# A decoder trunk on one core: gate evacuations ahead of recurrences, forget gate on ScalarE, scores times values first, the last norm later, two output rows stored first

## The chip, the cores and the metric

The kernel runs on one core of a Trainium2 chip, in one launch. The metric is the device time in microseconds (us) of one execution, as the median of several runs. PE is TensorE (PEld its weight loads), DVE is VectorE, ACT is ScalarE, POOL is GpSimd; SP issues nearly all DMAs.

## The reference

Sequence 2048, width 1024, batch 1, one layer, float32:

```python
proj = (rms_norm(x) * (1 + sc1) + sh1) @ w_in          # 3856 columns, cut into groups of heads:
#   retention (4 heads), HGRN2 (8 heads), GLA (4 heads); each a chunkwise recurrence, chunks of 64
f     = lb + (1 - lb) * sigmoid(z)                     # HGRN2: forget gate
key   = (1 - lb) * sigmoid(-z)                         # HGRN2: key
o     = (scores * causal decay) @ v + (q * decay) @ S  # per chunk: inside the chunk, and from the state S
S     = decay * S + (k * decay).T @ v
o     = rms_norm(o) per head * silu(gate)
x     = x + g1 * (concat(o) * head_gain @ w_out)
h     = rms_norm(x) * (1 + sc2) + sh2
u     = causal_conv3(h @ w_up)                         # 2 x 2816 columns
x     = x + g2 * ((silu(u_gate) * u_val) @ w_down)
out   = rms_norm(x) * final_gain
```

The scales sc, shifts sh and gates g come from a conditioning vector.

## The kernel before

Features lie on the partitions, tokens on the free axis. Matmuls are full precision by three passes: each operand is split into a high and a low part (`high` and `low`, `split`: a CAST on ACT, then a subtraction on DVE), and `split3` multiplies high by high, high by low, low by high; in the profile these are L254, L255 and L256. (In the changed kernel every line from here on has a number one to ten higher.)

**Token mixer.** Four blocks b = 0..3 of 512 tokens. In each, seven units follow one another: four of HGRN2 (`unit_h`, h0 to h3, tiles named like `kh1_3` for block 1, unit 3), one of GLA (`unit_g`), two of retention (`unit_r`). A unit is projections (`cf_gemm`, `tf_gemm`, `tf512`: tiles `psh..`, `psvg..`, `psqkvgr`), their evacuation from PSUM to SBUF by ACT and DVE, and then a recurrence (`gated`, `retention`), whose small matmuls are spread between the projections of later units. For HGRN2 `sf` and `sn` are the two sigmoids, `f` the forget gate, `kq` the key (tile `kh`), `sq` the silu of q (`sqh`), `v`/`sg` value and silu gate (`tok_evac`, `tok_evac4`, tiles `vh`, `sgh`, `sgg`). The recurrence scales q and k level by level (`qbh`, `kh`, `eh`), makes scores (`lvh`, `ath`), the output `oh` (`attn_out`: state product first, then scores times values, chunk by chunk) and updates states `S` from `uh`. For the retention units the scores are `scrr` and `atr`, the output `or`.

The next block's norm is three parts: `norm1_stat` sums squares (`san`), `rstd` transposes the sum by PE (`ssn`), takes the inverse root on DVE with three Newton rounds (12 tiny operations, `rsn`) and broadcasts it by PE (`bcn`), and `norm1_h` scales the rows (`xn`) and splits them into `ha`. After the mixer `out_half` and `out_finish` multiply by w_out (tiles `y`), add to the residual rows `x1` and make the second norm (`n2`), whose rows go to DRAM as `h2d`. For the last block these rows are normed in place: the four two-row buffers (`xy`) of `x1_3` are stored and then pass to the FFN.

**FFN.** Two super-blocks of 1024 tokens, with seven products instead of eight in each 2 x 2 split (Strassen's scheme). `up_stage` makes for each of 22 column groups f the products into PSUM tiles X, Y, Z (operands `A` from weights, `B` from features, the last-made ones `hB`/`lB`), adds them up to `uv` and `ug` (a ring `u` of three buffers), takes the convolution (`yv`, `yg` in the four `xy` buffers) and the gate. `up_second` of group f is issued inside group f+1. `down_stage` multiplies by w_down; `down_norm` makes the final norm of a half, and then scales and stores row by row; rows `y` 6 and 7 of half 0 lie in buffers (`t2s`) that the next super-block's weights also use.

**What sets the order.** PE executes in the order in which the program issues its matmuls. That order is made by `Clock`: each projection moves a clock on (`adv`), and generators and callbacks (`at(us, fn)`, `chain(gen, us)`) are run when it reaches their due time. So a number such as 14.0 says after how much PE work something is issued. The order on DVE, ACT and the queues is made by a scheduler that goes by priorities: `tc.high_priority(offset=...)` puts instructions ahead by that much; HOT is 600, CHAIN is 400. On each engine the order is then fixed, and an instruction waits for its operands and holds up all behind it.

## Time and profile before

| | us |
|---|---|
| median of 3 runs | 2531.41 (2528.41 to 2534.57) |
| profiled execution, its own time | 2533.2 |
| its span (first to last instruction) | 2531.4, mean granted clock 0.992 |
| PE busy | 2452.0 (97%) |
| DVE busy | 1989.5 (79%) |
| ACT busy | 1147.5 (45%) |
| POOL busy | 146.3 (6%) |

The mixer takes the first 1240 us or so, the up stage of super-block 0 begins there. A wait in the profile is put down to the instruction that ended it. Stretches are given in us from the start of the span. A group line reads: line, engine, operation, out<-in, count, then busy us, mean ns of one, and idle time ahead of it. "PEclk" or granted clock is 1.00 at full speed.

### The profile page before, as it was taken

The numbers are of one execution on the slowest core, as the hardware profiler recorded it, in microseconds if no ns is written. First come the engines' busy times: TensorE is split into PE (matmuls) and PEld (weight loads), VectorE is DVE, ScalarE is ACT, GpSimd is POOL, SyncE is SP. The second block draws the span as 40 slices with busy tenths as digits, with TensorE's granted clock in tenths as the row PEclk, the third lists the DMA queues.
The fourth block names the chain that finished last, engine by engine and source line by source line (L and its number), as shares of the span: only waits on it lengthen the run. The fifth ranks groups of instructions, "written<-read, shape, count | busy, mean of one in ns | idle before, by whom it ended". The sixth has DMA issues, their size and how long they took to land.

```text
span 2531.4 us, 35178 instructions
## 1 busy us (share of the span) xinstructions
PE 2452.0 (97%) x12165; PEld 2059.3 (81%) x12165; DVE 1989.5 (79%) x3652; ACT 1147.5 (45%) x1950; POOL 146.3 (6%) x278
## 2 busy tenths in 40 slices
PE   5999999999999999999999999999989999999998
PEld 4888877888888888788788888888868888888887
DVE  8987887877688685877798888887678777778666
ACT  3334434434443434434554454455445545545442
POOL 1000000000000000000100000000001010010000
PEclk9999999999999999999999999999999999999999
DMA  8844458865689647884654544587665544447663
GB/s 312 296 159 134 169 169 322 290 234 169 215 283 318 224 157 241 311 300 158 222 190 147 171 147 141 168 283 243 209 199 186 159 137 152 150 133 263 213 196 126
DMA packets 232498, 525.11 MB, mean 207 GB/s; under 512 B 24928, under 2 KB 28032, under 8 KB 232320
## 3 DMA queue, kind: packets, MB, share of 16 engines
q1 hardware_dynamic: 229120, 512.38, 60.0%
q0 software_dynamic: 3200, 10.49, 1.2%
q8 instruction: 96, 1.57, 0.2%
q14 instruction: 82, 0.67, 0.1%
HBM read 397.46 MB, written 125.30 MB: 207 GB/s over the span
## 4 chain that ended last, share of the span: by engine, by line
PE 82%; DVE 8%; DMA 5%; issue 2%; ACT 1%; SPq 0%; DVEq 0%; POOL 0%; ACTq 0%; POOLq 0%
PE X L254 6%; PE X L256 6%; PE X L255 6%; PE Z L256 3%; PE Z L255 3%; PE Z L254 3%; PE lvh L662 3%; PE dX L256 3%; PE dX L255 3%; PE dX L254 3%; PE psqkvgr L254 2%; PE psqkvgr L256 2%; PE psqkvgr L255 2%; PE y L254 2%; PE y L256 2%
## 5 line engine op out<-in xcount | busy, mean ns | idle before, releaser
L254 PE MATMUL X<-B,A 128*128 128x512 f32 x572 | 224.4, 392 | 1.4 <-ACT u L1354 1.4
L255 PE MATMUL X<-B,A 128*128 128x512 f32 x572 | 223.9, 391 | 0.0
L256 PE MATMUL X<-B,A 128*128 128x512 f32 x572 | 223.6, 391 | 0.0
L1055 DVE TENSOR_TENSOR dA<-rd,dA 128x512 fp32r<-128x512 f32 x154 | 106.0, 689 | 87.6 <-ACT dA L1054 87.5
L1054 ACT CAST dA<-rd 128x512 fp32r<-128x512 f32 x154 | 95.6, 621 | 138.8 <-PE dY L256 42.2
L1055 DVE TENSOR_TENSOR A<-s,A 128x512 fp32r<-128x512 f32 x176 | 120.7, 686 | 40.7 <-ACT A L1054 40.3
L1054 ACT CAST A<-s 128x512 fp32r<-128x512 f32 x176 | 108.6, 618 | 68.0 <-PE Z L256 45.2
L254 PE MATMUL dX<-dB,dA 128*128 128x512 f32 x352 | 136.9, 389 | 0.0
L255 PE MATMUL dX<-dB,dA 128*128 128x512 f32 x352 | 136.9, 389 | 0.0
L256 PE MATMUL dX<-dB,dA 128*128 128x512 f32 x352 | 136.9, 389 | 0.0
L254 PEld LDWEIGHTS X<-B,A 128*128 128x128 f32 x572 | 108.2, 189 | 24.5 <-ACT u L1354 2.2
L255 PEld LDWEIGHTS X<-B,A 128*128 128x128 f32 x572 | 108.2, 189 | 22.7
L256 PEld LDWEIGHTS X<-B,A 128*128 128x128 f32 x572 | 108.2, 189 | 22.7
L255 PE MATMUL Z<-B,A 128*128 128x512 f32 x308 | 120.0, 390 | 2.2 <-DVE B L1055 2.2
L254 PE MATMUL Z<-B,A 128*128 128x512 f32 x308 | 119.9, 389 | 0.0
L256 PE MATMUL Z<-B,A 128*128 128x512 f32 x308 | 119.8, 389 | 0.0
L662 PEld LDWEIGHTS lvh<-qbh,kh 128*128 128x128 f32 x768 | 100.5, 192 | 17.0 <-issue 9.2
L1055 DVE TENSOR_TENSOR dB<-rb,dB 128x512 fp32r<-128x512 f32 x154 | 105.6, 686 | 10.2 <-ACT dB L1054 10.1
L1055 DVE TENSOR_TENSOR A<-r,A 128x512 fp32r<-128x512 f32 x130 | 89.3, 687 | 29.4 <-ACT A L1054 29.1
L662 PE MATMUL lvh<-qbh,kh 128*128 128x128 f32 x768 | 102.8, 277 | 7.3 <-DVE kh L672 7.1
L1054 ACT CAST A<-r 128x512 fp32r<-128x512 f32 x130 | 81.0, 623 | 62.4 <-PE Z L256 60.0
L254 PE MATMUL psqkvgr<-hqkvgr,ha 128*128 128x512 f32 x256 | 106.1, 415 | 1.1 <-DVE orsg L160 1.0
(475 smaller groups left out, 6981.2 us busy)
## 6 DMA issues: line engine op xcount, KB each, us to landing
gs<-yv SPq DMA_DIRECT2D x154, 256.0 KB, 2.9
rb<-gs SPq DMA_DIRECT2D x154, 256.0 KB, 3.9
r<-wup SPq DMA_DIRECT2D x140, 256.0 KB, 3.3
s<-sumsu SPq DMA_DIRECT2D x136, 256.0 KB, 3.0
wada<-wada SPq DMA_DIRECT2D x48, 512.0 KB, 6.0
rd<-sumsd SPq DMA_DIRECT2D x88, 256.0 KB, 3.8
rd<-wdown SPq DMA_DIRECT2D x66, 256.0 KB, 3.9
x<-xT SPq DMA_DIRECT2D x64, 256.0 KB, 5.8
```

Of the source, the lines that this page charges most:

```text
L254: T.matmul(ps, lhs[0], rhs[0], start=first, stop=False, skip_group_check=more)
L255: T.matmul(ps, lhs[0], rhs[1], start=False, stop=False, skip_group_check=more)
L256: T.matmul(ps, lhs[1], rhs[0], start=False, stop=last, skip_group_check=more)
L662: T.matmul(ps[:, c * P:(c + 1) * P].rearrange("p (h n s) -> p h n s", h=2, s=s), kq[:, c * P:(c + 1) * P], rhs, start=True, stop=True)
L1054: S.copy(hi, src)
L1055: V.tensor_tensor(lo, src, hi, op=ALU.subtract)
```

## The change

1. The evacuations of projections (values, gates, the q sigmoid and its multiply, GLA's and retention's copies) get priority HOT.
2. `f` and `kq` of `unit_h` are made by ACT (a scaled activation each) instead of DVE: 32 instructions move.
3. `attn_out` multiplies scores by values for all chunks first, then adds the state products.
4. `norm1_h` gets priority CHAIN, and `norm1_stat` issues its sum after 20 us of PE work instead of 14.
5. The recurrence chains of `unit_h` begin after 9 (unit 0 of blocks 0 and 1) or 7 instead of 9 (block 0, unit 0) or 6.
6. For the last block, the squares of the second norm get priority -100 instead of 600, and the sum is issued at 20 instead of 5.
7. `down_norm` scales and stores rows 6 and 7 first in half 0, and the broadcast comes after 9 or 13 instead of 8 or 10.

```diff
+LATER = 100
...
         # norm1_stat
-                clock.at(14.0, rstd(acc[0], f"n1_{b}", bc1[b][:], lambda: done.add(("n1", b)), gap=9.5))
+                clock.at(20.0, rstd(acc[0], f"n1_{b}", bc1[b][:], lambda: done.add(("n1", b)), gap=9.5))
...
         # norm1_h
-            scaled(t[:], bc1[b][:], k)
-            high(t[:], k, f"{b}_")
-            low(t[:], k)
+            with tc.high_priority(offset=CHAIN):
+                scaled(t[:], bc1[b][:], k)
+                high(t[:], k, f"{b}_")
+                low(t[:], k)
...
         # tok_evac, and in the same way tok_evac4, sf and sn, sq, al, kq, qs and z of unit_g, a of unit_r
-            S.copy(v[:, c2, :], p3[:, :, 0:P])
-            S.activation(sg[:, c2, :], p3[:, :, P:256], AF.Sigmoid)
-            V.tensor_tensor(sg[:, c2, :], sg[:, c2, :], p3[:, :, P:256], op=ALU.mult)
+            with tc.high_priority(offset=HOT):
+                S.copy(v[:, c2, :], p3[:, :, 0:P])
+                S.activation(sg[:, c2, :], p3[:, :, P:256], AF.Sigmoid)
+                V.tensor_tensor(sg[:, c2, :], sg[:, c2, :], p3[:, :, P:256], op=ALU.mult)
...
         # attn_out
         for c in range(NCH):
-            oc = ps[:, c * P:(c + 1) * P]
-            inter = not (b == 0 and c == 0)
-            if inter:
-                T.matmul(oc, qn[:, c * P:(c + 1) * P], Sst[:, (b * NCH + c) % NS, :], start=True, stop=False)
             for hh in range(2):
-                T.matmul(oc[:, hh * 64:hh * 64 + 64], attn[:, (c * 2 + hh) * P:(c * 2 + hh + 1) * P],
-                         v[:, c, hh * 64:hh * 64 + 64], start=not inter, stop=hh == 1 if inter else True)
+                T.matmul(ps[:, c * P + hh * 64:c * P + hh * 64 + 64], attn[:, (c * 2 + hh) * P:(c * 2 + hh + 1) * P],
+                         v[:, c, hh * 64:hh * 64 + 64], start=c == hh == 0, stop=False, skip_group_check=True)
+        for c in range(1 if b == 0 else 0, NCH):
+            T.matmul(ps[:, c * P:(c + 1) * P], qn[:, c * P:(c + 1) * P], Sst[:, (b * NCH + c) % NS, :],
+                     start=False, stop=c == NCH - 1, skip_group_check=True)
...
         # unit_h
-        V.tensor_scalar(f[:], sf[:], oml[:, u:u + 1], lb[:, u:u + 1], op0=ALU.mult, op1=ALU.add)
-        V.tensor_scalar(kq[:], sn[:], oml[:, u:u + 1], None, op0=ALU.mult)
+        S.activation(f[:], sf[:], AF.Identity, scale=oml[:, u:u + 1], bias=lb[:, u:u + 1])
+        S.activation(kq[:], sn[:], AF.Copy, scale=oml[:, u:u + 1])
...
-        clock.chain(gated(nm, b, u, pos, kq, decay, subs, xy), 9.0 if b == u == 0 else 6.0)
+        clock.chain(gated(nm, b, u, pos, kq, decay, subs, xy), 9.0 if u == 0 and b < 2 else 7.0)
...
         # out_half
-                    with tc.high_priority(offset=HOT):
+                    with tc.high_priority(offset=HOT if b < NB - 1 else -LATER):
                         sumsq(acc, x1[m], m, f"n2_{b}_")
...
         # out_finish
-        clock.at(5.0, rstd(acc, f"n2_{b}", bc[:], then, gap=9.5))
+        clock.at(5.0 if b < NB - 1 else 20.0, rstd(acc, f"n2_{b}", bc[:], then, gap=9.5))
...
         # down_norm
-        def then(m=0):
+        def then(n=0):
+            m = (n - 2) % KD if h == 0 else n
...
-        clock.at(7.0 if h else 12.0, rstd(acc, f"n3_{b}", bc[:], then, bank=bank, gap=8.0 if h else 10.0))
+        clock.at(7.0 if h else 12.0, rstd(acc, f"n3_{b}", bc[:], then, bank=bank, gap=9.0 if h else 13.0))
```

Three places show how it moves instructions. The first is DVE in unit h3 of block 0, around 174 us of the trace. Here `kg`, `qbg`, `atg` are GLA's recurrence, `eh0_2` and `fh0_2` the decays of unit h2, `san` the sum of squares for the next block. Before:

```order
L626 TENSOR_TENSOR eh0_2_1441<-fh0_2_1440 128x128
L359 TENSOR_TENSOR san1_1_1450<-san1_1_1450,sqn1_1_5_1646 128x512
L626 TENSOR_TENSOR eh0_2_1441<-eh0_2_1441 128x64
L744 TENSOR_SCALAR fh0_3_1629<-sfh0_3_1689,oml_89,lb_90 128x512
L626 TENSOR_TENSOR eh0_2_1441<-eh0_2_1441 128x32
L745 TENSOR_SCALAR kh0_3_1628<-snh0_3_1690,oml_89 128x512
L626 TENSOR_TENSOR eh0_2_1441<-eh0_2_1441 128x16
L359 TENSOR_TENSOR san1_1_1450<-san1_1_1450,sqn1_1_6_1705 128x512
L626 TENSOR_TENSOR eh0_2_1441<-eh0_2_1441 128x8
L749 TENSOR_TENSOR sqh0_3_1771<-pshqh0_3_1708,sqh0_3_1771 128x512
L626 TENSOR_TENSOR eh0_2_1441<-eh0_2_1441 128x4
```

and after:

```order
L360 TENSOR_TENSOR san1_1_1450<-san1_1_1450,sqn1_1_5_1646 128x512
L759 TENSOR_TENSOR qbh0_2_1615<-sqh0_2_1606,fh0_2_1440 64x512 x2
L317 TENSOR_TENSOR lvgh0_3_2_1900<-rvgh0_3_2_1897,hvgh0_3_2_1899 128x1024
L754 TENSOR_TENSOR sqh0_3_1771<-pshqh0_3_1708,sqh0_3_1771 128x512
L673 TENSOR_TENSOR qbg0_0_1156<-qbg0_0_1156,eg0_991 128x64x8
L673 TENSOR_TENSOR qbg0_1_1165<-qbg0_1_1165,eg0_991 128x64x8
L675 TENSOR_TENSOR kg0_989<-kg0_989,eg0_991 128x32x8
L684 COPY_PREDICATED atg0_0_1590<-m_all_87,lvg0_8_1756 128x64x8
L684 COPY_PREDICATED atg0_1_1592<-m_all_87,lvg0_8_1761 128x64x8
L629 TENSOR_TENSOR eh0_2_1441<-fh0_2_1440 128x128
L360 TENSOR_TENSOR san1_1_1450<-san1_1_1450,sqn1_1_6_1705 128x512
L629 TENSOR_TENSOR eh0_2_1441<-eh0_2_1441 128x64
```

The multiply `sqh0_3`, which is what empties its PSUM bank, stood behind the decay chain `eh0_2` and the last GLA scores, and now stands ahead of both, and f and kh of unit h3 (L744, L745) are gone from this engine.

The second is DVE at the border from block 1 to block 2, around 584 us: `S3_110` is the state of unit h3, which PE reads for `oh1_3`; `xn2`, `ha2` are the next block's rows; `x1_1_0` a residual row; `ra1r` and `kkr` belong to retention. Before:

```order
L365 SCALAR_TENSOR_TENSOR xn2_0_5507<-xn2_0_5507,mod_104,bc1_2_4662 128x512
L853 TENSOR_TENSOR ra1r1_1_5444<-ra1r1_1_5444,rb1r1_1_5446 128x8x32
L854 TENSOR_TENSOR ra1r1_1_5444<-ra1r1_1_5444,rb1r1_1_5446 128x8x32
L372 SCALAR_TENSOR_TENSOR ha2_0_5510<-xn2_0_5507,mod_104,ha2_0_5510 128x512
L711 SCALAR_TENSOR_TENSOR S3_110<-S3_110,eh1_3_4444,uh1_3_5596 64x64
L986 SCALAR_TENSOR_TENSOR x1_1_0_5561<-y1_0_1_5586,mod_104,x1_1_0_5561 128x512
L711 SCALAR_TENSOR_TENSOR S3_110<-S3_110,eh1_3_4444,uh1_3_5596 64x64 x7
L365 SCALAR_TENSOR_TENSOR xn2_1_5513<-xn2_1_5513,mod_104,bc1_2_4662 128x512
```

and after:

```order
L714 SCALAR_TENSOR_TENSOR S3_110<-S3_110,eh1_3_4444,uh1_3_5593 64x64 x2
L366 SCALAR_TENSOR_TENSOR xn2_0_5507<-xn2_0_5507,mod_104,bc1_2_4662 128x512
L366 SCALAR_TENSOR_TENSOR xn2_1_5513<-xn2_1_5513,mod_104,bc1_2_4662 128x512
L996 SCALAR_TENSOR_TENSOR x1_1_0_5561<-y1_0_1_5586,mod_104,x1_1_0_5561 128x512
L366 SCALAR_TENSOR_TENSOR xn2_2_5519<-xn2_2_5519,mod_104,bc1_2_4662 128x512
L373 SCALAR_TENSOR_TENSOR ha2_0_5510<-xn2_0_5507,mod_104,ha2_0_5510 128x512
L373 SCALAR_TENSOR_TENSOR ha2_1_5516<-xn2_1_5513,mod_104,ha2_1_5516 128x512
L373 SCALAR_TENSOR_TENSOR ha2_2_5522<-xn2_2_5519,mod_104,ha2_2_5522 128x512
L714 SCALAR_TENSOR_TENSOR S3_110<-S3_110,eh1_3_4444,uh1_3_5593 64x64 x6
L866 TENSOR_TENSOR kkr1_1_5233<-ra1r1_1_5444,c_all_86 128x512
```

The first two of eight state updates come ahead of the rows of the next block now, and seven 128x512 operations stand between them and the other six.

The third is the beginning of the up stage, around 1262 us. On PE, `bcn2_3` is the broadcast of the last block's second norm. Before:

```order
L255 MATMUL Z0_0_11726<-B0_3_1_11713,A0_0_3_11624 128x512
L256 MATMUL Z0_0_11726<-B0_3_1_11713,A0_0_3_11624 128x512
L348 MATMUL bcn2_3_11872<-c_all_86,rsn2_3_11767 128x128 x4
L254 MATMUL Z0_0_11726<-B0_3_2_11718,A0_0_3_11624 128x512
L255 MATMUL Z0_0_11726<-B0_3_2_11718,A0_0_3_11624 128x512
L256 MATMUL Z0_0_11726<-B0_3_2_11718,A0_0_3_11624 128x512
```

and after:

```order
L255 MATMUL X0_2_11988<-B0_1_3_11012,A0_2_1_11950 128x512
L256 MATMUL X0_2_11988<-B0_1_3_11012,A0_2_1_11950 128x512
L257 MATMUL X0_2_11988<-B0_1_3_11012,A0_2_1_11950 128x512
L349 MATMUL bcn2_3_12010<-c_all_86,rsn2_3_11899 128x128 x4
L255 MATMUL X0_1_11810<-B0_4_0_11688,A0_1_4_11803 128x512
L256 MATMUL X0_1_11810<-B0_4_0_11688,A0_1_4_11803 128x512
L257 MATMUL X0_1_11810<-B0_4_0_11688,A0_1_4_11803 128x512
```

It stood in product 3 of column group 0 (`Z0_0`), and now stands behind a product of group 2 and ahead of product 4 of group 1 (`X0_1`, 12 matmuls), which product 3 of group 1 (`Z0_1`) follows. On DVE at the same place, `x1_3` are the normed rows, `yv0_0` and `yg0_0` the convolution of group 0, `ug0_1` the sum that reads `Z0_1`. Before:

```order
L1055 TENSOR_TENSOR A0_2_6_12005<-s1_0_2_11995,A0_2_6_12005 128x512
L1011 SCALAR_TENSOR_TENSOR x1_3_4_11200<-x1_3_4_11200,mod_104,bc2_3_11661 128x512 x2
L1011 SCALAR_TENSOR_TENSOR x1_3_6_11304<-x1_3_6_11304,mod_104,bc2_3_11661 128x512
L1055 TENSOR_TENSOR A0_2_5_12008<-s0_0_2_11994,A0_2_5_12008 128x512
L1011 SCALAR_TENSOR_TENSOR x1_3_6_11304<-x1_3_6_11304,mod_104,bc2_3_11661 128x512
L1277 TENSOR_TENSOR s2_0_2_11996<-r00_0_2_11984,r10_0_2_11998 128x512
L1289 SCALAR_TENSOR_TENSOR yv0_0_11917<-uv0_0_11727,vec_84,yv0_0_11917 128x1024
L1055 TENSOR_TENSOR A0_2_7_12012<-s2_0_2_11996,A0_2_7_12012 128x512
L1290 SCALAR_TENSOR_TENSOR yv0_0_11917<-uv0_0_11727,vec_84,yv0_0_11917 128x1024
L1280 TENSOR_TENSOR s3_0_2_11997<-r01_0_2_11986,s1_0_2_11995 128x512
L1355 TENSOR_TENSOR ug0_1_11834<-Z0_1_11832,u3_0_1_11839 128x512
```

and after:

```order
L1065 TENSOR_TENSOR A0_3_2_12157<-r01_0_3_12152,A0_3_2_12157 128x512
L1021 SCALAR_TENSOR_TENSOR x1_3_0_11041<-x1_3_0_11041,mod_104,bc2_3_11661 128x512 x2
L1021 SCALAR_TENSOR_TENSOR x1_3_2_11095<-x1_3_2_11095,mod_104,bc2_3_11661 128x512 x2
L1021 SCALAR_TENSOR_TENSOR x1_3_4_11191<-x1_3_4_11191,mod_104,bc2_3_11661 128x512
L1065 TENSOR_TENSOR A0_2_3_11981<-s3_0_2_11959,A0_2_3_11981 128x512
L1021 SCALAR_TENSOR_TENSOR x1_3_4_11191<-x1_3_4_11191,mod_104,bc2_3_11661 128x512
L1021 SCALAR_TENSOR_TENSOR x1_3_6_11304<-x1_3_6_11304,mod_104,bc2_3_11661 128x512 x2
L1299 SCALAR_TENSOR_TENSOR yv0_0_11859<-uv0_0_11727,vec_84,yv0_0_11859 128x1024
L1300 SCALAR_TENSOR_TENSOR yv0_0_11859<-uv0_0_11727,vec_84,yv0_0_11859 128x1024
L1299 SCALAR_TENSOR_TENSOR yg0_0_11865<-ug0_0_11728,vec_84,yg0_0_11865 128x1024
L1365 TENSOR_TENSOR ug0_1_11814<-Z0_1_11812,u3_0_1_11819 128x512
```

The rows stand in one piece directly ahead of the convolution, with one operand split among them, and `ug0_1` stands behind one more step of the convolution.

## The prediction

> **What bounds the kernel now.** I read the page first, then the waits of PE, then stretches around each wait, then single instructions. All times are those of the profiled execution: 2533.2 us, of which the span is 2531.4 and 1.8 lie around it. The median of the runs is 2531.41, 1.8 below it, so I form the change against 2533.2 and take the same difference off the median.

> ```profile
> PE 2452.0 (97%) x12165; PEld 2059.3 (81%) x12165; DVE 1989.5 (79%) x3652; ACT 1147.5 (45%) x1950; POOL 146.3 (6%) x278
> PE 82%; DVE 8%; DMA 5%; issue 2%; ACT 1%; SPq 0%; DVEq 0%; POOL 0%; ACTq 0%; POOLq 0%
> ```

> PE works 2452.0 of 2531.4 us and no matmul is added or removed, so all that can change is the 79 us in which PE is not busy, and the stretches in which its clock is halved. The waits of PE (waiting instruction <- releaser: us in total, times, longest us; the 14.6, 3.9, 3.7 and 2.7 of the startup are left out, the change doesn't touch them):

> ```profile
> PE lvh L662 <- DVE kh L672: 7.1, 6, 3.8
> PE X L254 <- ACT A L1054: 6.2, 2, 5.1
> PE pshfh L254 <- DVE sgg L561: 4.5, 1, 4.5
> ...
> PE psvgh L254 <- DVE sqh L749: 3.7, 1, 3.7
> PE X L254 <- ACT hB L1054: 2.7, 1, 2.7
> ...
> PE ssn L337 <- DVE S L711: 2.6, 1, 2.6
> ...
> PE Z L255 <- DVE B L1055: 2.2, 1, 2.2
> PE bcn L348 <- DVE rsn L160: 2.0, 1, 2.0
> PE pshfh L255 <- DVE ha L372: 1.9, 1, 1.9
> ...
> PE psqkvgr L254 <- DVE orsg L160: 1.0, 1, 1.0
> ...
> PE alg L790 <- DVE sgh L561: 0.6, 1, 0.6
> ```

> Each is one place, except kh (six). The stretches around them, with the busy time of PE, PEld, DVE, ACT and POOL, then the granted clock:

> ```profile
> 172.00:186.00 14.00, 10.34 (x42) 8.68 (x41) 11.85 (x26) 1.68 (x2) 0.00 (x0) 0.76 0.43 141
> 300.00:314.00 14.00, 12.11 (x58) 10.15 (x56) 9.56 (x28) 5.45 (x8) 1.04 (x2) 0.88 0.42 142
> 340.00:350.00 10.00, 6.53 (x32) 6.02 (x33) 9.01 (x18) 0.84 (x2) 0.00 (x0) 0.83 0.33 107
> 578.00:600.00 22.00, 22.00 (x125) 19.12 (x124) 21.05 (x56) 11.11 (x19) 2.08 (x4) 1.00 0.73 244
> 600.00:880.00 280.00, 277.08 (x1532) 237.19 (x1530) 213.70 (x509) 116.11 (x223) 9.38 (x18) 1.00 0.71 244
> 880.00:900.00 20.00, 20.00 (x133) 18.16 (x132) 19.01 (x46) 10.07 (x17) 2.08 (x4) 1.00 0.51 174
> 1040.00:1052.00 12.00, 7.55 (x25) 5.75 (x24) 8.02 (x24) 2.95 (x11) 0.00 (x0) 0.72 0.76 256
> 1246.00:1262.00 16.00, 13.29 (x46) 10.06 (x47) 11.49 (x29) 8.43 (x16) 3.36 (x6) 0.79 0.61 204
> 1860.00:1900.00 40.00, 31.12 (x130) 23.79 (x129) 28.87 (x63) 13.68 (x24) 5.17 (x11) 0.96 0.58 191
> ```

> Two things are to be seen. A wait costs more than itself: the clock falls after it, and length times (1 - clock) is lost besides, 14 x 0.24 = 3.4 us at 172, 12 x 0.28 = 3.4 at 1040, 16 x 0.21 = 3.4 at 1246, 1.7 at 300 and at 340, 1.6 at 1860. And at the borders between blocks (578 to 600, 880 to 900) PE is 100% busy while DVE is busy 96% and 95%: there is no wait, and no room on DVE for one to be avoided.

> **What the change takes away.** *At 177* the gate multiply sqh is late:

> ```profile
> 170.88 0.60 ACT L748 ACTIVATE sqh<-pshqh 128x512 f32<-128x512 f32 x1
> 176.36 0.69 DVE L749 TENSOR_TENSOR sqh<-pshqh,sqh 128x512 f32<-128x512 f32 x1
> 177.10 0.80 PE L254 MATMUL psvgh<-hvgh,ha 128*128 128x512 f32 x1 [3.66 <-DVE sqh L749]
> ```

> Its sigmoid ended at 171.5 and DVE came to it 4.9 us later; that held a PSUM bank that PE needs. At priority HOT it stands ahead of the recurrence work. The wait of 3.7 and the 3.4 of clock go: **-7.0**. *At 1045* sgg holds a bank in the same way (12.00 - 7.55 = 4.45, and 3.4): **-7.8**. *At 1886* an activation tile of the next super-block is cast late because its buffer still holds rows 6 and 7 of the output, stored last; now they go first. Idle in 1860 to 1900 is 40.00 - 31.12 = 8.9, of it 2.0 the norm's wait (its broadcast comes some 3 us later, so that goes too); I leave 0.7, and 1.6 of clock goes: **-9.8**. *At 309* 1.9 + 1.7: **-3.6**. *At 343* (kh, 3.5 and 1.7) DVE is 9.01 of 10 busy and only about 1 us of its work leaves for ACT, so of a possible 5.2 I take **-1.0**. *The smaller ones* (S 2.6, orsg 1.0, the other five of kh 7.1 - 3.8 = 3.3, and 0.6) have either later steps on PE or earlier ones on DVE: 7.5, of which I take **-6.5**. Sum: -35.7.

> **Forget gate and key on ScalarE.**

> ```profile
> L744 DVE TENSOR_SCALAR fh<-sfh,oml,lb 128x512 f32<-128x512 f32 x16 | 8.7, 542 | 3.1 <-ACT sfh L742 3.0
> L1012 ACT ACTIVATE x<-x,mod 128x512 f32<-128x512 f32 x8 | 5.7, 720 | 1.2 <-DVE x L1011 1.1
> ```

> Sixteen f (0.54 each) leave DVE, and sixteen kh of nearly the same length, some 16 us in all. The nearest row for them on ACT is a scaled ACTIVATE of the same shape, 0.72: 32 x 0.72 = 23 us on an engine that is 45% busy, with no more tables to load. Their wait is bounded by 0 and by 16 x (0.72 - 0.54) = 3; I take 0, since the chain behind them is DVE work that is queued anyway. Scores times values first costs PE no instruction and moves the read of the state some 2 us later in each chunk group; nothing by itself.

> **What the change puts in.** *Borders.* norm1_h of the next block is at CHAIN now, so its 16 DVE operations (xn, ha) stand ahead of what PE waits for there: the last states S, and the retention scores.

> ```profile
> L372 DVE SCALAR_TENSOR_TENSOR ha<-xn,mod,ha 128x512 fp32r<-128x512 f32 x24 | 17.7, 745 | 0.2
> 585.68 2.16 DVE L711 SCALAR_TENSOR_TENSOR S<-S,eh,uh 64x64 f32<-64x64 f32 x7
> 586.55 0.38 PE L594 MATMUL oh<-S,qbh 128*128 128x128 f32 x2
> 598.20 0.69 DVE L903 TENSOR_TENSOR atr<-scr,c_all 128x512 f32<-128x512 f32 x1
> 600.25 0.38 PE L594 MATMUL or<-S,qnr 128*128 128x128 f32 x2
> ```

> Before, PE read S while the updates ran, and the second half of atr ended 1.4 us ahead of its reader. Now seven 128x512 operations (six of norm1_h, one of the residual; some 0.66 each as they overlap, 4.6 in all) stand between the second update of S and the third, and the rest of norm1_h ahead of atr. Two operations that stood ahead of S are gone (1.3), so the states come about 3 us after PE wants them, and atr about 3 more: 6.0 at 580 to 605. At the next border 4.4 in the same count, at the first 3.7 (which gives back the 3.6 of 309). The price of a border lies between 0, if DVE has caught up by then, and 16 x 0.66 = 10.6; I take the counts: 3.7 + 6.0 + 4.4 = **+14.1**, and the clock twice 1.7: **+3.4**.

> *Norm sums of blocks 1 and 2* (at 14, now 20): each broadcast moves to where its Newton steps or a PSUM bank aren't ready yet. On PE the first stands behind eight state products and waits for the updates that free its bank (2.9), the second follows its sum by too little for twelve small DVE operations that share DVE with weight sums (4.5). The measured norm wait is 2.0, so from 0 to some 5 each; **+7.4**, with 1.7 of clock.

> *Sum of squares of the last block at -LATER.* The squares hold tiles in which the split of the last feature rows (hB) is put; hB is ready some 8 us late instead of 4.9 (2.7 + 2.2): **+3.1**.

> *The last block's norm at 20 instead of 5* is the dearest. The chain behind its broadcast, in the trace (start, length; the line of h2d is of the DMA issues, its last number the time to landing):

> ```profile
> 1262.60 0.60 PE L348 MATMUL bcn<-c_all,rsn 128*128 128x128 f32 x4
> 1263.24 0.58 ACT L349 COPY bc<-bcn 128x512 f32<-128x512 f32 x1 [0.17 <-PE bcn L348]
> 1266.26 1.41 DVE L1011 SCALAR_TENSOR_TENSOR x<-x,mod,bc 128x512 f32<-128x512 f32 x2
> h2d<-x SPq DMA_DIRECT2D x8, 256.0 KB, 3.1
> 1271.22 1.25 ACT L1288 ACTIVATE yv<-uv,vec 128x1024 f32<-128x1024 f32 x1
> 1273.30 1.28 DVE L1289 SCALAR_TENSOR_TENSOR yv<-uv,vec,yv 128x1024 f32<-128x1024 f32 x1
> 1277.56 0.68 DVE L1355 TENSOR_TENSOR ug<-Z,u 128x512 f32<-128x512 f32 x1
> 1280.84 0.39 PE L254 MATMUL Z<-B,A 128*128 128x512 f32 x1
> ```

> The four xy buffers hold the residual rows; yv0_0 can take one when two rows are normed and stored; ug0_1 can take its buffer of the ring u (three) when the convolution of yv0_0 has read it; product 3 on PE may overwrite Z0_1 only when ug0_1 has read it. From broadcast to product 3 there were 1280.84 - 1262.60 = 18.2 us. In the new order there is the broadcast (0.4) and one product of 12 matmuls (2.7) between: 3.1 us. The chain needs: broadcast and copy 1.2, two rows on DVE 1.5, ACT's half of the second 0.8, the store 3.1, yv 1.25, two convolution steps 2.6, the first of yg that now stands ahead of ug 1.3, ug 0.7, together about 12.5. So PE waits 9.4, and the clock takes 1.7 to 3.4: **+11.7**. Between 0 (the buffers free without the stores) and 12.5 + 3.4.

> *The tail.* Broadcast gap 9 instead of 8, with the twelve Newton steps among the row multiplies: **+2.5**. At the start the modulation job may wait 1: **+1**.

> Sum of what is put in: 14.1 + 3.4 + 9.1 + 3.1 + 11.7 + 3.5 = 44.9. Net 44.9 - 35.7 = +9. Gains are single measured waits, losses are counts that ignore DVE work done while PE waits; I shade the losses by 3: **+6, to 2539 profiled, 2537 as a median.**

> [...] The clock first by rows: after a wait of only 1.9 (300 to 314) the clock was 0.88, after the one of 2.6 (in 600 to 880) it stayed 1.00. [...]

> **Rivals.** *(a) Faster: DVE covers the borders.* If PE waits at the earlier places anyway, or the 1 us per unit that left DVE lets it arrive early, S and atr are ready. What decides is whether DVE is at norm1_h more than some 4 us earlier than before, relative to PE. For it: block by block DVE loses 4 us of work. Against: 96% and 95% busy at the borders, and PE loses its waits too. Then 17.5 and the norm sums' 9.1 fall away: 44.9 - 26.6 = 18.3, net -17, 2514. *(b) Faster: the last norm's chain is shorter.* If yv0_0 needs no stored row, the 11.7 is gone: with the shading -5.5, 2526. Against it: in the order yv0_0 waits for two of these stores. *(c) Slower by more: every new wait draws 3.4 of clock,* as the rows of 172, 1040 and 1246 did. Six new waits over 2.5 at 1.7 more each are +10, and no shading +3: 2550. [...] *(e) The reorder does nothing:* excluded, as the two orders differ at all these places.

> **How the numbers follow.** Forecast of 2532 to 2543: 0.38. (a) 0.15, (b) 0.17, (c) 0.15, (d) 0.15. 0.2% is 5 us, and about what a measurement of this kernel can tell from no change. Slower (over 2536.5): 0.33 of the forecast and (c), 0.48. Same: (d) and the forecast's low end, 0.20. Faster: (a), (b), 0.32. The range leaves out a tenth at each end: 2514 to 2553.

> **What would show it.** In the profile after: no wait for sqh near 177, for sgg near 1045, nor for A at 1886; waits of PE for S and atr at three borders (right if 2 to 6 each); a wait of Z or X on ug near 1290 of about 9, the longest after the startup; hB later than before by 3. The prediction is wrong if the wait on ug is under 4, or if the borders show no wait: then the time is under 2525.

## The result, and the profile after

The changed kernel takes 2568.39 us (median of 4 runs, 2565.89 to 2570.10), the kernel before 2532.99 (4 runs): a ratio of 1.0140, 95% interval 1.0119 to 1.0160. It is 35 us slower where 6 were forecast, and outside the range of 2514 to 2553. One run of the kernel before, among those beside the experiments, took 9262 us at a granted clock of 0.41 and is left out of the ratios.

The page after, the engines' busy time and then the shares of the chain of work that ended last:

```profile
PE 2468.1 (96%) x12165; PEld 2073.0 (81%) x12165; DVE 1977.4 (77%) x3620; ACT 1168.1 (45%) x1982; POOL 146.9 (6%) x278
PE 78%; DVE 9%; DMA 7%; issue 3%; ACT 2%; SPq 0%; POOL 0%; DVEq 0%; ACTq 0%; POOLq 0%
```

The span grew from 2531.4 to 2567.8, by 36.4. PE does the same 12165 matmuls, yet is busy 16.1 us longer (2452.0 to 2468.1). That is the halved clock (granted 0.50): between 60 and 2500 us it stands for 64.9 us in this trace and for 30.7 in the one before, and half of the difference is 17.1. The other 20.3 are idle time of PE (79.4 to 99.7). DVE gave up 12.1 us and ACT, with 18 table loads in both traces, took 20.6; what that is worth is tested below.

The waits of PE after (total, times, longest):

```profile
PE Z L255 <- DVE ug L1365: 10.2, 1, 10.2
PE lvh L665 <- DVE kh L675: 8.9, 7, 2.4
PE X L255 <- ACT u L1360: 6.2, 1, 6.2
...
PE or L596 <- DVE atr L913: 5.3, 2, 3.5
PE oh L599 <- DVE S L714: 4.7, 2, 3.1
PE bcn L349 <- DVE rsn L161: 4.6, 1, 4.6
...
PE X L255 <- ACT m L1351: 3.8, 1, 3.8
...
PE og L596 <- DVE S L714: 3.5, 1, 3.5
PE X L255 <- ACT hB L1064: 2.8, 1, 2.8
PE bcn L349 <- DVE S L714: 2.4, 1, 2.4
```

The waits on sqh and sgg are gone. New, and forecast, are those on ug, S, atr and the norm's two broadcasts. Three were not forecast: og on S, m on ACT, and at the first border kh, where S and atr were expected:

```profile
281.31 1.97 PE L665 MATMUL lvh<-qbh,kh 128*128 128x128 f32 x8 [2.40 <-DVE kh L675]
```

The waits on kh were to shrink from 7.1 and grew to 8.9: those at 422, 432 and 1002 of the trace before went, and those at 281, 288 and 833 came.

The stretches around them (length, busy of PE, PEld, DVE, ACT, POOL, granted clock, then the DMA engines' share and GB/s):

```profile
170.00:186.00 16.00, 16.00 (x91) 13.83 (x90) 14.47 (x29) 3.99 (x8) 0.00 (x0) 1.00 0.39 132
200.00:212.00 12.00, 9.60 (x55) 8.08 (x55) 6.71 (x24) 1.13 (x3) 0.00 (x0) 0.86 0.25 89
276.00:300.00 24.00, 21.05 (x105) 17.51 (x104) 20.24 (x35) 9.35 (x14) 0.00 (x0) 0.93 0.62 210
496.00:512.00 16.00, 12.49 (x75) 11.21 (x74) 12.59 (x41) 3.71 (x6) 1.25 (x3) 0.89 0.80 286
524.00:540.00 16.00, 11.40 (x52) 9.57 (x51) 8.95 (x24) 2.33 (x3) 0.00 (x0) 0.79 0.89 287
596.00:626.00 30.00, 24.76 (x134) 22.04 (x134) 24.31 (x63) 12.57 (x21) 2.09 (x4) 0.89 0.34 112
900.00:930.00 30.00, 24.94 (x137) 22.23 (x136) 23.79 (x59) 13.12 (x21) 2.08 (x4) 0.89 0.32 111
1040.00:1066.00 26.00, 25.56 (x141) 21.57 (x141) 21.95 (x46) 15.24 (x28) 1.04 (x2) 1.00 0.76 277
1262.00:1284.00 22.00, 12.91 (x42) 9.41 (x41) 15.96 (x26) 11.84 (x23) 2.19 (x4) 0.77 0.65 227
1304.00:1324.00 20.00, 9.82 (x31) 7.54 (x30) 16.73 (x21) 12.28 (x18) 2.00 (x4) 0.66 0.50 174
1914.00:1930.00 16.00, 11.96 (x43) 8.92 (x42) 12.76 (x24) 7.62 (x14) 2.32 (x5) 0.79 0.56 180
```

Since PE's matmuls are the same, each can be matched with itself in the two traces (by tile and order of occurrence), and the difference of its two starting times says where the time goes. A step in that difference is the cost of a place, its wait and its clock together:

| place (time before) | forecast | measured |
|---|---|---|
| sqh, 177 | -7.0 | -6.7 |
| broadcast of block 1, 205 | +2.9 | +4.5 |
| border 0 to 1, 280 | +3.7 | +5.1 |
| ha, 309 | -3.6 | -2.7 |
| kh, 343 | -1.0 | -0.6 |
| og on S, 500 | 0 | +4.1 |
| broadcast of block 2, 521 | +4.5 | +7.6 |
| border 1 to 2, 580 to 620 | +6.0 | +9.4 |
| border 2 to 3, 880 to 900 | +4.4 | +9.2 |
| sgg, 1045 (with orsg, 1111) | -8.8 | -7.4 |
| split of the last rows, 1250 | +3.1 | +4.5 |
| last norm's chain, 1285 | +11.7 | +13.8 |
| output rows and norm, 1867 to 1900 | -9.8 | -4.2 |
| tail | +2.5 | +2.0 |

The forecast column has no clock for the borders and the two broadcasts; it had 3.4 and 1.7 for all of them together. Small places, -2.3 together, make up the rest of +36.3. These times come from one execution of each kernel.

The dearest place, on PE, ACT and DVE in turn (start, length):

```profile
1302.85 0.60 PE L349 MATMUL bcn<-c_all,rsn 128*128 128x128 f32 x4
1304.10 0.59 ACT L350 COPY bc<-bcn 128x512 f32<-128x512 f32 x1
1304.85 3.40 DVE L1021 SCALAR_TENSOR_TENSOR x<-x,mod,bc 128x512 f32<-128x512 f32 x5
1310.17 1.23 ACT L1298 ACTIVATE yv<-uv,vec 128x1024 f32<-128x1024 f32 x1
1311.48 1.28 DVE L1299 SCALAR_TENSOR_TENSOR yv<-uv,vec,yv 128x1024 f32<-128x1024 f32 x1 [0.65 <-issue]
1314.43 1.28 DVE L1299 SCALAR_TENSOR_TENSOR yg<-ug,vec,yg 128x1024 f32<-128x1024 f32 x1 [0.35 <-ACT yg L1298]
1315.64 0.68 DVE L1365 TENSOR_TENSOR ug<-Z,u 128x512 f32<-128x512 f32 x1
1316.37 0.80 PE L255 MATMUL Z<-B,A 128*128 128x512 f32 x1 [10.18 <-DVE ug L1365]
```

From broadcast to product 3 it took 13.5 us, of which PE had 3.3 of work. The first matmul of product 3, in the last line, takes 0.80 instead of 0.39: the clock is halved for 13.65 us from 1308.8.

### The profile page after: what moved, and what is told of

It is laid out like the page before. It is cut to its first block, busy times and chain, and to the rows that moved or that the text cites. A ratio compares the mean times of both kernels' runs of the same rounds, so it can differ in the third digit from the quotient of the medians.

```text
span 2567.8 us, 35177 instructions
## 1 busy us (share of the span) xinstructions
PE 2468.1 (96%) x12165; PEld 2073.0 (81%) x12165; DVE 1977.4 (77%) x3620; ACT 1168.1 (45%) x1982; POOL 146.9 (6%) x278
## 4 chain that ended last, share of the span: by engine, by line
PE 78%; DVE 9%; DMA 7%; issue 3%; ACT 2%; SPq 0%; POOL 0%; DVEq 0%; ACTq 0%; POOLq 0%
PE X L255 6%; PE X L256 6%; PE X L257 6%; PE dX L255 3%; PE dX L257 3%; PE dX L256 3%; PE Z L255 3%; PE Z L257 3%; PE Z L256 3%; PE lvh L665 3%; PE psqkvgr L255 2%; PE psqkvgr L257 2%; PE psqkvgr L256 2%; PE dY L257 2%; PE dY L255 2%
## 5 line engine op out<-in xcount | busy, mean ns | idle before, releaser
L255 PE MATMUL X<-B,A 128*128 128x512 f32 x572 | 224.5, 392 | 1.7 <-ACT u L1364 1.7
L255 PE MATMUL dX<-dB,dA 128*128 128x512 f32 x352 | 136.9, 389 | 0.0
L255 PE MATMUL Z<-B,A 128*128 128x512 f32 x308 | 121.0, 393 | 10.2 <-DVE ug L1365 10.2
L255 PEld LDWEIGHTS X<-B,A 128*128 128x128 f32 x572 | 108.1, 189 | 25.0 <-ACT u L1364 2.9
L1064 ACT CAST A<-r 128x512 fp32r<-128x512 f32 x130 | 81.0, 623 | 64.9 <-PE Z L257 63.4
L255 PE MATMUL psqkvgr<-hqkvgr,ha 128*128 128x512 f32 x256 | 107.2, 419 | 0.0
## 6 DMA issues: line engine op xcount, KB each, us to landing
gs<-yv SPq DMA_DIRECT2D x154, 256.0 KB, 2.9
rb<-gs SPq DMA_DIRECT2D x154, 256.0 KB, 3.9
r<-wup SPq DMA_DIRECT2D x140, 256.0 KB, 3.3
s<-sumsu SPq DMA_DIRECT2D x136, 256.0 KB, 3.0
rd<-sumsd SPq DMA_DIRECT2D x88, 256.0 KB, 3.8
rd<-wdown SPq DMA_DIRECT2D x66, 256.0 KB, 3.8
x<-xT SPq DMA_DIRECT2D x64, 256.0 KB, 6.2
```

The lines of the kernel that those rows point to most:

```text
L255: T.matmul(ps, lhs[0], rhs[0], start=first, stop=False, skip_group_check=more)
L1064: S.copy(hi, src)
```

## The experiments

My theory: each new wait is local, made by the one edit that moved what it waits for, and costs its idle time and what the clock loses behind it. The rivals: that the evacuations at HOT push the recurrences back everywhere, that ACT delays f and kh, or that DVE is behind anyway. All ratios are to the kernel before, run beside; the changed kernel's is 1.0140, and 0.1% is 2.5 us. Of the single edits on the changed kernel, only part 6 as a whole and norm1_h give intervals clear of its own (1.0119 to 1.0160). What is said of the others rests on the matched times of one execution each.

**The last block's norm (part 6) taken back.**

```diff
-                    with tc.high_priority(offset=HOT if b < NB - 1 else -LATER):
+                    with tc.high_priority(offset=HOT):
-        clock.at(5.0 if b < NB - 1 else 20.0, rstd(acc, f"n2_{b}", bc[:], then, gap=9.5))
+        clock.at(5.0, rstd(acc, f"n2_{b}", bc[:], then, gap=9.5))
```

> The changed kernel with its part 6 taken back (the last block's squares at HOT, its norm sum after 5 us). Theory (local waits: each new wait of PE is set by the one edit that moved what it waits for, and costs its idle time and half of the throttled time behind it): the waits at 1271 (6.2), 1278 (2.8) and 1316 (10.2) go back to the 4.9 that stood there before, and the throttled 13.65 and 6.8 with them; the stretch from 1250 to 1290 gave 18.0 us, so the time falls by 14 to 19, to 2549 to 2555. Rival (the chain of the xy buffers and the ring u is late for another reason, the gates and rows split by DVE that is behind): the wait on ug stays above 5 and less than 8 us come back.

1.0051 (1.0033 to 1.0068), some 22 us less. The three waits (19.1 together) are gone, and one of 3.3 on B is left. Matched with the changed kernel, the stretch itself gives 18.4, as expected. Another 6.6 come off ahead of it, where the waits are alike: at 205 both wait 2.4, but only the changed kernel's clock falls there (half clock for 3.41 us from 206.30; over the whole span 0.984 is granted against 0.991). It is the clock's luck, below.

**Its two halves apart.** First the squares at HOT again, with the sum still at 20:

```diff
-                    with tc.high_priority(offset=HOT if b < NB - 1 else -LATER):
+                    with tc.high_priority(offset=HOT):
```

> The changed kernel with the last block's squares at HOT again, its norm sum still issued after 20 us. Theory (two separate waits): the squares hold up the split of the last feature rows, so the waits at 1271 (6.2, on u behind hB on ACT) and 1278 (2.8, on hB) shrink to about 5 in all; the chain from the late broadcast is untouched, so the wait on ug at 1316 stays at 10.2, within 1. The time falls by 3 to 8 us, a ratio of 1.011 to 1.013. Rival (all three waits come from the late broadcast): neither of them shrinks by more than 1 us.

```profile
PE Z L255 <- DVE ug L1365: 10.2, 1, 10.2
PE Z L256 <- DVE B L1065: 3.5, 4, 2.7
```

1.0131 (1.0115 to 1.0147). These are the waits of this place now: those on u and hB (8.9) became 3.5 on B in four pieces, that on ug stayed. The stretch gives 5.4; 2.8 were lost ahead of it. So the low priority of the squares costs some 5 us, and the late broadcast the rest. Then the sum at 12, with the squares late:

```diff
-        clock.at(5.0 if b < NB - 1 else 20.0, rstd(acc, f"n2_{b}", bc[:], then, gap=9.5))
+        clock.at(5.0 if b < NB - 1 else 12.0, rstd(acc, f"n2_{b}", bc[:], then, gap=9.5))
```

> The changed kernel with the last block's norm sum issued after 12 us instead of 20 (the squares stay at -100). Now four products of 12 matmuls, 10.9 us, lie between the broadcast and product 3 that overwrites Z0_1, where the changed kernel has one (2.7). Theory (the chain from broadcast to ug takes 12.7 to 13.3 us whatever PE does): the wait on ug falls from 10.2 to 1 to 3, and the time by 9 to 15 us, a ratio of 1.008 to 1.0105. Rival (DVE or ACT are behind there anyway): the wait on ug stays over 5.

1.0109 (1.0092 to 1.0126), just over what was expected. The wait on ug is 3.8, not 1 to 3: with 10.9 us of products between, PE waits 3.8, with 2.7 it waits 10.2. From broadcast to product 3 it is 15.3 us here and 13.5 in the changed kernel; DVE does seven other operations within this chain here, sums and splits of operands, and two there. So the chain is not quite constant, but it is this chain that PE waits for. That the seven operations are what lengthens it is not shown by a run.

**norm1_h at its old priority.**

```diff
-            with tc.high_priority(offset=CHAIN):
-                scaled(t[:], bc1[b][:], k)
...
+            scaled(t[:], bc1[b][:], k)
```

> The changed kernel with norm1_h at its old priority. Theory (local waits): the waits for S and atr at the borders (281 to 300, 600 to 616, 905 to 921) go, 24.5 us by the aligned times; the wait for ha at 309 comes back (3.7). The time falls by 16 to 22, to 2546 to 2552. Rival (evacuations at HOT are what push the state updates and scores back): the border waits stay, and the time falls by less than 6.

1.0050 (1.0034 to 1.0067), some 23 us less; the waits of oh on S and of or on atr are gone, as is that on kh at the first border (kh in all 4.3 instead of 8.9), and the wait for ha (1.9) is back. The matched times give 5.1 at the first border, 9.3 and 9.1 at the others, and take 1.2 back at ha. The rival (HOT) is out for the borders: the evacuations were still at HOT.

**norm1_stat at 14 again.**

```diff
-                clock.at(20.0, rstd(acc[0], f"n1_{b}", ...
+                clock.at(14.0, rstd(acc[0], f"n1_{b}", ...
```

> The changed kernel with norm1_stat's sum issued after 14 us of PE work again instead of 20. Theory (local waits): the broadcast of block 1 (2.4 at 205, behind the bank that the state updates free) and that of block 2 (4.6 at 529, with 6.8 of half clock) come back to their old places, where there was no wait: 8 to 13 us less than the changed kernel, a ratio of 1.009 to 1.011 to the kernel before. Rival (the Newton steps are late because of the evacuations at HOT ahead of them, not because of the place of the sum): the waits move with the broadcast, and less than 4 us come back.

1.0117 (1.0100 to 1.0135). By the matched times 4.6 at 205 and 5.7 at 520, 10.3 as expected. The wait at 205 is gone, the one of 4.6 is 1.2, so something of the later Newton steps is due to the rest of the change. But the sum for block 3, issued earlier again, waits for S at 801, 2.6 as before the change, and with its clock that costs 4.3. So the later sum had a gain too, and 6.0 is what it cost in these places together; the median moved by 6.

**Broadcast gaps of the final norm at 8 and 10 again, rows 6 and 7 still first.**

```diff
-        clock.at(..., rstd(acc, f"n3_{b}", bc[:], then, bank=bank, gap=9.0 if h else 13.0))
+        clock.at(..., rstd(acc, f"n3_{b}", bc[:], then, bank=bank, gap=8.0 if h else 10.0))
```

> The changed kernel with down_norm's broadcast gaps at 8 and 10 again, rows 6 and 7 still first. Theory: the first rows are scaled some 3.5 us earlier, so the store and the load through the shared buffers end that much earlier, and the wait at 1921 (3.8, with 6.8 of half clock behind it) goes; the wait of the broadcast itself, 2.0 before, comes back. The time falls by 3 to 7. Rival (what PE waits for there is a copy on ACT that is late by itself): no more than 1 us.

1.0105 (1.0076 to 1.0135), but by the matched times only 3.1: 1.1 at this place, where the wait for the broadcast (1.1) is back, and 2.0 in the tail. PE still waits 3.4 for m. ACT there:

```profile
1915.06 0.62 ACT L1064 CAST A<-s 128x512 fp32r<-128x512 f32 x1 [6.05 <-DMA s<-sumsu]
...
1919.22 0.57 ACT L1351 COPY m<-X 128x512 f32<-128x512 f32 x1
```

The cast waits for its load, a weight sum of the next super-block. In the kernel before, the first such cast stood behind the copy m on ACT (m at 1881.52, the cast at 1885.33); now it stands ahead, and in the order of the engine it holds up squares, other casts and m. In the changed kernel it is so too, with less idle time:

```profile
1919.25 0.62 ACT L1064 CAST A<-s 128x512 fp32r<-128x512 f32 x1 [2.00 <-DMA s<-sumsu]
...
1920.30 0.58 ACT L1351 COPY m<-X 128x512 f32<-128x512 f32 x1
```

The buffer is filled earlier, but ACT now stands and waits for it. It is the row order that puts the cast ahead: undo4, below, has no other edit to the FFN and waits 3.5 for m, while the kernel with only the evacuations at HOT waits for A as before (4.1) and not for m. So the rival is right that PE waits for ACT, and not by itself: it is the same load.

**Final norm of half 0 earlier, on the kernel without the moves of the norms** (undo4, below):

```diff
-        clock.at(7.0 if h else 12.0, rstd(acc, f"n3_{b}", bc[:], then, bank=bank, gap=8.0 if h else 10.0))
+        clock.at(7.0 if h else 8.0, rstd(acc, f"n3_{b}", bc[:], then, bank=bank, gap=8.0 if h else 10.0))
```

> undo4 (the changed kernel without its moves of the norms) with the final norm of half 0 issued after 8 us of PE work instead of 12. Theory (in the changed kernel and in undo4 the first cast of the next super-block stands on ACT ahead of the copy m that PE needs, and waits for rows 6 and 7 to be stored and the buffer filled again; with the rows 4 us earlier it is there in time): the wait on m at 1872 (3.5, with 3.4 of half clock) goes, 3 to 6 us less than undo4, a ratio of 0.993 to 0.9945. Rival (the load is late because its queue is busy): the wait stays within 1 us.

0.9961 (0.9947 to 0.9974), no gain over undo4. The wait on m is gone, as the theory says, but two others stand there:

```profile
PE ssn L338 <- DVE n3a L360: 3.2, 1, 3.2
...
PE Y L255 <- DVE y L1520: 2.2, 1, 2.2
```

The sum of squares isn't ready so early. By the matched times 5.0 were lost ahead of the norm and 3.5 won behind it.

**The old order in attn_out.**

```diff
+            if inter:
+                T.matmul(oc, qn[:, c * P:(c + 1) * P], Sst[:, (b * NCH + c) % NS, :], start=True, stop=False)
             for hh in range(2):
...
-        for c in range(1 if b == 0 else 0, NCH):
```

> The changed kernel with the old order in attn_out (state product, then scores times values, chunk by chunk). Theory: the order is nearly free; it reads the states some 1 to 2 us later, so without it the waits on S at the borders grow by about 1 each and those on atr stay: 0 to 5 us slower than the changed kernel, a ratio of 1.014 to 1.016. Rival (scores first is what makes PE wait for atr at 615 and 921): these waits (5.3) go, and 4 to 9 us come back, 1.010 to 1.012.

1.0124 (1.0108 to 1.0141), 4 us less by the ratio and 4.7 by the matched times. The wait on atr at the second border fell from 3.5 to 2.5, and at the third from 1.8 to 1.3, while oh waits for S 1.6, 2.7 and 3.3. The rival has the sign, not the mechanism: waits only moved by a microsecond or so, and of the 4.3 us between the two spans 3.4 are PE busy time, that is, clock (granted 0.985 against 0.984). Whether the new order costs or gains stays open.

**f and kh on DVE again.**

```diff
-        S.activation(f[:], sf[:], AF.Identity, scale=oml[:, u:u + 1], bias=lb[:, u:u + 1])
-        S.activation(kq[:], sn[:], AF.Copy, scale=oml[:, u:u + 1])
+        V.tensor_scalar(f[:], sf[:], oml[:, u:u + 1], lb[:, u:u + 1], op0=ALU.mult, op1=ALU.add)
+        V.tensor_scalar(kq[:], sn[:], oml[:, u:u + 1], None, op0=ALU.mult)
```

> The changed kernel with f and kh on DVE again. Theory: DVE gets 1 us per unit back, which shows where it is the late one (kh, S, atr, Newton steps, 15 waits): 3 to 10 us slower than the changed kernel, a ratio of 1.015 to 1.018. Rival (f and kh are late now because ACT takes them in order behind evacuations, and that is where the waits on kh come from): the waits on kh get shorter, and the ratio is 1.009 to 1.012.

1.0148 (1.0130 to 1.0166), 2 us more by the ratio, just under what was expected, and 1 less in the trace by the matched times. The waits on kh fell from 8.9 to 6.1, as the rival says, but others stand in their place (`or` 2.9 at 345, `kTg` 3.8 at 498), and the time did not fall. Moving 12 us from DVE to ACT made no difference that these runs can tell.

**Only the evacuations at HOT, on the kernel before.**

```diff
         # as in part 1 of the change, in tok_evac, tok_evac4, unit_h, unit_g and unit_r; nothing else
+            with tc.high_priority(offset=HOT):
```

> The kernel before with only the evacuations at HOT. Theory: the waits on sqh (3.7), sgg (4.5) and 0.6 and the half clock behind the first two (6.8 us in all) go and nothing is put in: 10 to 16 us faster than before, 2517 to 2523. Rival (HOT evacuations push the recurrences back): waits for kh, S or atr take their place, and the time is within 4 us of before or above it.

0.9973 (0.9960 to 0.9985), 7 us faster, less than expected and more than the rival says. (The profiled execution was the slowest of ten, 4.4 above their median.) sqh and sgg give 6.7 and 6.8 by the matched times. But other waits stand in their place, so the rival is partly right:

```profile
PE lvh L665 <- DVE kh L675: 6.8, 4, 4.4
...
PE ssn L338 <- DVE S L714: 3.5, 1, 3.5
PE oTh L583 <- DVE oh L577: 3.3, 2, 2.9
PE bcn L349 <- DVE orsg L161: 3.2, 1, 3.2
```

The steps at 513 and at 758 to 800 cost about 13 together (the one at 799 stands in place of 2.6 before). Behind oh at 758 DVE had stood 3.4 us for the load of a weight sum that is now ahead of it.

**All four moves of the norms taken back.** This takes back parts 4, 6 and the gaps of 7; parts 1, 2, 3, 5 and the row order stay.

```diff
-                clock.at(20.0, rstd(acc[0], f"n1_{b}", ...
+                clock.at(14.0, rstd(acc[0], f"n1_{b}", ...
-            with tc.high_priority(offset=CHAIN):
-        clock.at(5.0 if b < NB - 1 else 20.0, rstd(acc, f"n2_{b}", ...
+        clock.at(5.0, rstd(acc, f"n2_{b}", ...
-                    with tc.high_priority(offset=HOT if b < NB - 1 else -LATER):
+                    with tc.high_priority(offset=HOT):
-        clock.at(..., rstd(acc, f"n3_{b}", bc[:], then, bank=bank, gap=9.0 if h else 13.0))
+        clock.at(..., rstd(acc, f"n3_{b}", bc[:], then, bank=bank, gap=8.0 if h else 10.0))
```

> The changed kernel without its moves of the norms: squares and sum of the last block, priority of norm1_h, place of norm1_stat's sum and the broadcast gaps of down_norm are as before; evacuations at HOT, f and kh on ACT, scores first, chain gaps and the row order stay. Theory (local waits add up): 22 (n2) + 22 (norm1_h) + 10 (norm1_stat) + 5 to 9 (gaps) go from the 35.5 that the changed kernel is slower: 24 to 28 us faster than before, a ratio of 0.989 to 0.991. Rival (the waits are shared: an edit taken away bares the wait of the next): 0.994 or more.

```profile
PE 2446.4 (97%) x12165; PEld 2055.8 (82%) x12165; DVE 1974.1 (78%) x3620; ACT 1166.5 (46%) x1982; POOL 147.3 (6%) x278
```

0.9953 (0.9936 to 0.9971): faster than both kernels, by 12 us against before, 47 against the changed one. PE is busy 2446.4, 21.7 less than in the changed kernel with the same 12165 matmuls, which is clock (granted 0.995 against 0.984). It is half of the gain expected, and by its figure (0.994 or more) the rival was right. The sums of single medians (22 + 23 + 6 + 9) counted clock that fell by luck; the four places by the matched times, 18.4 + 22.3 + 6.0 + 3.1 = 49.8, taken from 36.3, make -13.5, and the matched times of undo4 end at -16.7. (That execution was the fastest of four, 5.3 below the median.) So the places add up within some 3 us, and no wait over 1 us is bared that neither the kernel before nor the changed one has: the rival's figure came true, its mechanism is not seen.

**And the old begin of the recurrence chains on top of it.**

```diff
-        clock.chain(gated(nm, b, u, pos, kq, decay, subs, xy), 9.0 if u == 0 and b < 2 else 7.0)
+        clock.chain(gated(nm, b, u, pos, kq, decay, subs, xy), 9.0 if b == u == 0 else 6.0)
```

> undo4 with the recurrence chains of unit_h begun after 9 (block 0, unit 0) or 6 us again. Theory (the later begin gives kh time; what is left of the waits on kh at 332 and 336, 3.3, would grow): 0 to 5 us slower than undo4, a ratio of 0.995 to 0.9975. Rival (the later begin pushes state updates into the next unit, and is what makes PE wait for a bank at 492): that wait (2.6) goes, and 2 to 5 us come off.

0.9963 (0.9951 to 0.9975), the same as undo4. The wait on og (2.6 there) is gone, as the rival says, so the later begin made it, and most likely also the 3.5 us at 501 in the changed kernel:

```profile
501.72 1.52 PE L596 MATMUL og<-vg,atg 128*128 128x64 f32 x12 [3.51 <-DVE S L714]
```

The matmul that waits does not read S. The updates of GLA's states read `ug` from PSUM, so og probably waits for that bank; this is read off the operands and not tested. In its place kh waits 3.8 instead of 3.3, and a broadcast 2.9 instead of 1.2, so that nothing comes of it.

## Why the prediction was wrong

The sign, most places and the order of the costs were right: the waits on ug (10.2, forecast 9.4), on hB with u (8.9, forecast 8), on S and atr at two borders (at the first it was kh), on both broadcasts, and the end of those on sqh and sgg. The size was off by 30 us: 18.8 of clock and 11.3 of idle time. The step that failed most is the price of the clock behind the new waits. The terms, which overlap:

- **The clock.** The forecast had gains of 10.1 and losses of 7.4, 2.7 less in all; measured are 16.1 more. I gave 1.7 to two borders and one broadcast. In the trace a half clock of 3.4 us, which loses 1.7, stands at 206, 281, 346, 503, 906, 923 and 1278, one of 6.8 at 527, 616, 1268 and 1920, and of 13.65 at 1309. Rival (c) had the mechanism and at 2550 was too small as well: each new wait of 1.8 us or more drew clock, those of 1.5 (833) and 1.6 (600) did not.
- **Borders:** 14.1 forecast without clock, 23.7 measured with it. "I take the counts" held for the waits: at the first 3.0 against 3.7, though on kh, at the second 1.6 and 3.5 of idle time against 6.0, at the third 3.1 and 1.8 against 4.4. The excess is clock: at the second 5.1 of waits and 3.4 of clock make 8.5 of the 9.4.
- **Output rows first:** -9.8 forecast, -4.2 measured. Here "I leave 0.7" failed, where a wait of 3.8 and 3.4 of clock were left: I followed the cast, which was to come in time, and not what it moved ahead of on ACT: the copy m, which PE needs first.
- **og on S, 0 forecast, 4.1 measured.** The forecast has no term for the later begin of the chains. Without it this wait goes (2.6 on undo4).
- **The smaller waits** (S, five of kh, sgh): I took 5.5 of their 6.5 away, and orsg besides. That on S went, those on kh were replaced.
- **Shading the losses by 3** for DVE work that goes on while PE waits: nothing of that was seen. With their clock nearly all losses were larger than the counts.
- Right within 2.1: sqh, sgg, kh at 343, the last norm's chain, the squares, the tail. Rivals (a) and (b) are out by the trace of after, and (d), which has 0.15 of the chances, by the clock and the 35 us: no run shows that only waits over some length cost clock, and in the changed kernel half clock stood for 3.41 us from 923.10, behind a wait of 1.8.

## What to carry to other kernels

Cost an engine in order by what stands behind a waiting instruction, on each engine that the path crosses, and not only on the busiest. Ask what PE is about to read of an engine that is nearly full: at the second border, where PE was 100% busy and DVE 96% before, what was put ahead on DVE made PE wait 1.6 and 3.5 us, and cost 9.3 (undo_n1prio). Before a norm's broadcast is moved later, count the longest chain of buffers behind it: here it took 13.5 us from broadcast to product 3, and PE waited 10.2 of them. Where waits are short and many, compare single places by matching the same instructions in two traces: medians carry clock luck, here 60 us for four edits that gave 49.8 by the matched times.

## What the runs showed of the hardware

So in these two traces the clock that a wait cost went not by its length alone. In the kernel before, the wait for ha that ended at 308.96 is 1.89 long, lies in one piece, and half clock followed for 3.41 us; that for S that ended at 792.05 is 2.64 long, lies in two (1.13 and 1.51 us of idle time), and none followed. In the changed kernel the wait of 2.4 at 205 has 2.17 in one piece, and half clock followed. That is what is called luck above. The counts are of two executions of nearly the same kernel; no run shows what sets them, nor whether they hold for another.
